# Two heads' attention products in turns behind the later one, first query blocks joined, and the final norm's row spread two weight tiles into its expert

## The chip, the cores and the metric

The kernel runs on one core of a Trainium2 chip. TensorE (PE) multiplies matrices and accumulates in PSUM banks; VectorE (DVE) and ScalarE (ACT) empty the banks and do the elementwise work; the queues of SyncE (SP), ACT and GpSimd (POOL) issue the DMA transfers. The metric is the device time of one execution in microseconds; the median over several executions counts.

## What is computed

The input is 512 tokens of 1024 numbers in fp32. Two blocks follow each other. The first has two layers, of which the first is a causal attention with a forget gate, the second a gated linear recurrence; each is normed and followed by a gated projection. The second block has three mixers side by side, a long convolution, an attention over a neighbourhood on a grid and a pooling, and after them sixteen experts that each take the 64 tokens that score highest. A last norm with the gain `final_g` ends it. Cut to what the change touches:

```python
def fox_attention(q, k, v, c):            # 16 heads of 64, 512 positions
    def block(i):                         # query block of 128
        s = einsum('bhqd,bhkd->bhqk', qb, k) * scale
        s = s + (cb[..., :, None] - c[..., None, :])
        s = where(kpos <= qpos, s, -inf)
        w = softmax(s)
        return einsum('bhqk,bhkd->bhqd', w, v)
...
def neighbourhood_attention(q, k, v, rpb): # 8 heads of 64, grid of 8 rows by 64
    s = einsum('bchd,bicjhd->bhcij', q_row, k_nb) + bias   # 8 rows by 16 columns
    p = softmax(s over the neighbourhood)
    return einsum('bhcij,bicjhd->bchd', p, v_nb)
...
y = silu(xs @ w_gate[e]) * (xs @ w_up[e]) @ w_down[e]      # 16 experts
return rms_norm_2(x, final_g)
```

## The kernel before

**Dense projections.** `group` runs a projection in pieces. Weights and inputs are split into two numbers each, and `mm3` (L326 to L330) issues three products of 128 by 512 for each pair of tiles into one of four accumulator banks `acc`. `group` has an argument `fill`: a list of steps that are called between its products, evenly spread. All attention work stands in such lists. Engines run their instructions in program order; a scheduler of the framework sets that order, by the priority that code written earlier has and by when it thinks operands and buffers are ready. `high_priority` and `issue_after` steer it.

**First attention (`fox_body`).** Heads go in pairs, head a = 0 on partitions 0 to 63 and a = 1 on 64 to 127. For each pair and each of four query blocks, `unit(b, i)` (L577) takes two score banks `sc`, issues three products for head 0, then three for head 1 (L591), adds the causal mask through one product each (L594), and then for each head: DVE adds the bias row `cb` and finds the maximum (L599), ACT takes the exponential (L600), DVE the reciprocal and the scaling (L601, L602). The bias rows come by DMA on ACT's queue at the pair's first unit, into two buffers. `turn` (L605) transposes the weights `so` into a bank `pt` (L615) and ACT copies them out (L617). `avs` (L619) multiplies with the values for both heads, four products each of 512 down to 128 columns (L624), and DVE copies the bank `oT` out. `heads` (L629) makes steps of this: step k holds unit k, `avs` of a pair whose last turn is done, and the turn of unit k - 1. Two lists of four pairs are spread over five projections (L656 to L664).

**Second attention (`second_body`, L1072).** `na(b, jp)` (L1108) does one unit from end to end, for two heads and two of four column groups: four score products in two banks (L1115), then for each head in turn the bias addition with maximum (L1126), the sign (L1128), the exponential (L1130), the reciprocal (L1131), the scaling (L1133), four transposes (L1137), ACT's copy `pt` (L1139), and four products with the values (L1143), two halves of 128 positions for each of two column groups. DVE copies the bank `oN` to `YN` (L1147). Four of the eight units fill the projection `qk1`; the other four follow after two mixers' outputs are scaled and split (`into`), so that they lie beside the products of the output projection.

**Experts (`moe_body`).** A weight tile is 2 MB. `load` (L1448 to L1467) issues the tiles on SP's queue; the first twelve go to buffers that the mixers before leave free one by one, then a ring of them is refilled as each tile is used. `up(e)` (L1577) uses eight tiles, gate (`g`) and up (`u`) in alternation (L1587); behind the last product of tile `at`, counted from 0, it hangs small work: from `at` 4 the `scatter` of the expert before (`st`, L1648, added to the tokens' rows by DVE, L1649), and in expert 14 at 5 and 6 `gains` (L1633), which spreads one half of the row final_g over 128 partitions by a product with ones (`fg`, L1637) into a bank that `scatter` also uses. `down` (L1620) has the products with the third matrix. The last expert's products of that kind are issued in quarters (L1695).

## Time and profile before

| | |
|---|---|
| median of 3 executions | 1881.55 us (1879.29 to 1884.54) |
| the profiled execution | 1878.07 us, its span 1876.3 us |
| mean granted TensorE clock | 0.996 |
| busy: PE, DVE, ACT | 1818.5 us (97%), 846.6 us (45%), 494.6 us (26%) |
| DMA traffic | 496.94 MB, mean 265 GB/s |
| chain that ended last | PE 80%, DMA 13%, DVE 5% |

The profile is of one execution. The span runs from the first to the last instruction. Busy time is the sum of an engine's instructions; the records of PE overlap each other, so that starts are the better measure of its pace. A window row gives the busy time of each engine in a stretch with the number of instructions, then the granted clock and the DMA engines' mean share; with a tile, of that tile's instructions alone. In a timeline the number behind x says how many records one row joins, and a bracket tells idle time just before and what ended it.

### The profile page before, as it was taken

The numbers are of one execution on the slowest core, as the hardware profiler recorded it, in microseconds if no ns is written. First come the engines' busy times: TensorE is split into PE (matmuls) and PEld (weight loads), VectorE is DVE, ScalarE is ACT, GpSimd is POOL, SyncE is SP. The second block draws the span as 40 slices with busy tenths as digits, with TensorE's granted clock in tenths as the row PEclk, the third lists the DMA queues.
The fourth block names the chain that finished last, engine by engine and source line by source line (L and its number), as shares of the span: only waits on it lengthen the run. The fifth ranks groups of instructions, "written<-read, shape, count | busy, mean of one in ns | idle before, by whom it ended". The sixth has DMA issues, their size and how long they took to land.

```text
span 1876.3 us, 21770 instructions
## 1 busy us (share of the span) xinstructions
PE 1818.5 (97%) x8672; PEld 1036.2 (55%) x8672; DVE 846.6 (45%) x1946; ACT 494.6 (26%) x869; POOL 23.5 (1%) x37
## 2 busy tenths in 40 slices
PE   9999999999999999999999999999999989999897
PEld 6767677888888888776743333333333332333232
DVE  6464667774735574767532213333212331133212
ACT  6454644462434454235401000000000000000002
POOL 0000000000000000000100000000000000000000
PEclk9999999999999999999999999999999999999999
DMA  5322143322221337333899999999999999999995
GB/s 167 111 79 90 57 132 132 101 96 90 65 70 57 113 97 242 102 113 104 319 413 403 422 428 428 426 428 429 427 428 426 428 428 428 428 426 428 428 419 187
DMA packets 61403, 496.94 MB, mean 265 GB/s; under 512 B 7161, under 2 KB 8313, under 8 KB 36459
## 3 DMA queue, kind: packets, MB, share of 16 engines
q1 hardware_dynamic: 51908, 470.46, 62.1%
q10 hardware_dynamic: 7592, 18.70, 3.0%
q0 software_dynamic: 1792, 6.29, 1.1%
q8 instruction: 70, 1.15, 0.2%
q14 instruction: 41, 0.34, 0.1%
HBM read 491.20 MB, written 4.23 MB: 264 GB/s over the span
## 4 chain that ended last, share of the span: by engine, by line
PE 80%; DMA 13%; DVE 5%; ACT 1%; issue 1%; SPq 0%; ACTq 0%; DVEq 0%
PE acc L328 12%; PE acc L329 11%; PE acc L330 11%; DMA w<-mu 11%; PE y L1627 10%; PE u L1587 8%; PE g L1587 7%; PE gx L1539 3%; PE st L1648 2%; DMA w<-mg 1%; PE hT L1614 1%; PE oT L624 1%; PE sc L591 1%; PE pt L615 1%; PE oT L779 1%; PE oN L1143 1%
## 5 line engine op out<-in xcount | busy, mean ns | idle before, releaser
L328 PE MATMUL acc<-xhi,whi 128*128 128x512 f32 x800 | 318.2, 401 | 0.7 <-ACT xhi L323 0.7
L1649 DVE TENSOR_TENSOR H<-H,st 128x512 f32<-128x512 f32 x120 | 78.1, 683 | 522.0 <-PE st L1648 522.0
L330 PE MATMUL acc<-xhi,wlo 128*128 128x512 f32 x800 | 313.3, 393 | 0.0
L329 PE MATMUL acc<-xlo,whi 128*128 128x512 f32 x784 | 308.2, 393 | 0.2 <-DVE xlo L324 0.2
L1587 PE MATMUL g<-w,xt 128*64 128x512 f32 x1024 | 261.7, 598 | 11.2 <-DMA w<-mg 11.1
L1587 PE MATMUL u<-w,xt 128*64 128x512 f32 x1008 | 246.9, 596 | 8.7 <-DMA w<-mu 8.3
L306 DVE TENSOR_TENSOR wlo<-wraw,whi 128x1024 fp32r<-128x1024 f32 x127 | 155.1, 1222 | 180.9 <-ACT whi L305 159.7
L1627 PE MATMUL y<-w,ZH 128*64 128x512 f32 x944 | 222.9, 594 | 0.0
L305 ACT ACTIVATE whi<-wraw 128x1024 fp32r<-128x1024 f32 x127 | 134.2, 1057 | 210.8 <-PE acc L329 141.1
L1587 PEld LDWEIGHTS g<-w,xt 128*64 128x64 f32 x1024 | 79.9, 137 | 165.6 <-issue 137.9
L328 PEld LDWEIGHTS acc<-xhi,whi 128*128 128x128 f32 x800 | 150.4, 188 | 36.1 <-issue 3.4
L330 PEld LDWEIGHTS acc<-xhi,wlo 128*128 128x128 f32 x800 | 150.6, 188 | 31.8 <-issue 1.6
L329 PEld LDWEIGHTS acc<-xlo,whi 128*128 128x128 f32 x784 | 147.5, 188 | 32.1 <-issue 3.6
L1587 PEld LDWEIGHTS u<-w,xt 128*64 128x64 f32 x1008 | 74.3, 137 | 152.2 <-issue 129.1
L1627 PEld LDWEIGHTS y<-w,ZH 128*64 128x64 f32 x944 | 69.4, 137 | 130.5 <-issue 128.7
L1604 ACT ACTIVATE gs<-g 128x512 f32<-128x512 f32 x32 | 19.1, 597 | 389.9 <-PE g L1587 361.1
L1539 PE MATMUL gx<-res,oh 128*64 128x256 f32 x512 | 62.3, 385 | 10.8 <-DVE H L1649 10.8
L1571 ACT ACTIVATE ZH<-ogT 128x512 f32<-128x512 f32 x16 | 9.6, 597 | 228.0 <-PE ogT L1569 228.0
L1648 PE MATMUL st<-ZH 64*128 64x512 f32 x240 | 67.7, 641 | 0.0
L328 PE MATMUL acc<-whi,xhi 128*128 128x512 f32 x160 | 64.5, 404 | 0.0
L330 PE MATMUL acc<-whi,xlo 128*128 128x512 f32 x160 | 62.8, 392 | 0.0
L329 PE MATMUL acc<-wlo,xhi 128*128 128x512 f32 x160 | 62.8, 392 | 0.0
(510 smaller groups left out, 1934.8 us busy)
## 6 DMA issues: line engine op xcount, KB each, us to landing
w<-mg SPq DMA_DIRECT2D x63, 2048.0 KB, 32.2
w<-mu SPq DMA_DIRECT2D x62, 2048.0 KB, 31.2
w<-md SPq DMA_DIRECT2D x59, 2048.0 KB, 35.1
wraw<-wg SPq DMA_DIRECT2D x115, 512.0 KB, 3.5
w<-md SPq DMA_DIRECT2D x16, 512.0 KB, 10.8
cb<-cd ACTq DMA_DIRECT2D x16, 256.0 KB, 3.6
wraw<-wg POOLq DMA_DIRECT2D x8, 512.0 KB, 3.8
nab<-nab ACTq DMA_DIRECT2D x12, 256.0 KB, 2.9
```

What stands on the lines that cost most here:

```text
L305: self.last = nc.scalar.activation(hi, w, AF.Copy)
L306: nc.vector.tensor_sub(lo, w, hi.bitcast(F32))
L328: mm(out, wh, xh, start=start, stop=False)
L329: mm(out, wh, xl, start=False, stop=False)
L330: mm(out, wl, xh, start=False, stop=stop)
L591: nc.tensor.matmul(ss[a][:, :n], x[sl, i * 128:n], y[sl, :n], start=y is kh and x is qh, stop=False, skip_group_check=True)
L1539: nc.tensor.matmul(Q[w][t * 64:t * 64 + 64, :256], oh[:, i, :], rv[:, i, t, w], start=i == 0, stop=i == 3, skip_group_check=True)
L1587: mm = nc.tensor.matmul(A[b][t * 64:t * 64 + 64, :], xt[:, 2 * i + k, :], w[:, c:c + 512], start=at < 2 and k == 0, stop=at > 5 and k == 1 ...
L1604: nc.scalar.activation(g, G[b], AF.Silu)
L1627: nc.tensor.matmul(Y[t * 64:t * 64 + 64, :], hT[:, i % 2 * 4 + k, i // 2, :], w[:, k, t * 512:t * 512 + 512], start=kk == 0, stop=kk == 15 ...
L1648: nc.tensor.matmul(q, OHT[e][sl, i * 128:i * 128 + 128], YY[e][sl, :], start=True, stop=True)
L1649: V.tensor_add(total[:, i, t * 512:t * 512 + 512], total[:, i, t * 512:t * 512 + 512], q)
```

## The change

A new helper `pairs` takes a list of products, issues the first, and the rest only behind it. Both attentions now list the products of two heads alternately, head 1 first; softmax and transposes go through head 0 first.

In the first attention, query blocks 0 and 1 are one unit: block 0 takes the first 128 columns of a bank, block 1 the next 256; one mask product covers both diagonal squares. A pair has three units, a list of four pairs 14 steps where it had 18, and the lists are cut anew over the projections. Softmax and transposes still go by head and block, one at a time.

In the second attention `na` is cut in three: `scores`, `turn` and `values`. Step k issues the scores of unit k, the values of unit k - 2 and the transposes of unit k - 1; the values' eight products are one list over both heads. `so` lies in the tiles `t2` (five buffers) and no longer in one of its own (two). There are ten steps; 4 and 5 now stand between the two `into` of the first half of the output projection.

`gains` is called in expert 14 behind tiles 1 and 2, and no longer behind 5 and 6.

```diff
+    def pairs(self, todo):
+
+        mm = self.nc.tensor.matmul
+        (a, k), *todo = todo
+        first = mm(*a, skip_group_check=True, **k)
+        with self.tc.issue_after(first.ins):
+            for a, k in todo:
+                mm(*a, skip_group_check=True, **k)
+
...
+        STEPS = (0, 1), (2,), (3,)
+
+        def unit(b, g):
 
             (qh, ql), (kh, kl) = QT[b], KT_[b]
-            n = 128 * (i + 1)
...
             ss = [self.sc(), self.sc()]
-            for a in range(2):
-                sl = slice(a * 64, a * 64 + 64)
-                for x, y in ((qh, kh), (qh, kl), (ql, kh)):
-                    nc.tensor.matmul(ss[a][:, :n], x[sl, i * 128:n], y[sl, :n], start=y is kh and x is qh, stop=False,
-                                     skip_group_check=True)
-            for a in range(2):
-                nc.tensor.matmul(ss[a][:, i * 128:n], self.identb, self.cmask, start=False, stop=True, skip_group_check=True)
+            at = {i: 128 * (i - STEPS[g][0]) for i in STEPS[g]}
+            todo = []
+            for x, y in ((qh, kh), (qh, kl), (ql, kh)):
+                for i in STEPS[g]:
+                    n = 128 * (i + 1)
+                    for a in (1, 0):
+                        sl = slice(a * 64, a * 64 + 64)
+                        todo.append(((ss[a][:, at[i]:at[i] + n], x[sl, i * 128:n], y[sl, :n]), dict(start=y is kh and x is qh and i == STEPS[g][0], stop=False)))
+            self.pairs(todo)
+            for a in (1, 0):
+                if g == 0:
+                    nc.tensor.matmul(ss[a].rearrange("p (j k) -> p j k", k=128)[:, 0:3:2, :], self.identb,
+                                     self.cmask[:, None, :].to_broadcast([128, 2, 128]), start=False, stop=True, skip_group_check=True)
+                else:
+                    nc.tensor.matmul(ss[a][:, g * 128 + 128:g * 128 + 256], self.identb, self.cmask, start=False, stop=True, skip_group_check=True)
             with self.tc.high_priority():
                 for a in range(2):
-                    so = fp.tile([128, 512], F32, name="so", tag="so", bufs=4)
-                    st = fp.tile([128, 4], F32, name="st", tag="st", bufs=6)
-                    nc.vector.tensor_tensor_reduce(so[:, :n], ss[a][:, :n], CB[b][a][:, :n], 1.0, 3.0e38, OP.add, OP.min, st[:, 0:1])
-                    nc.scalar.activation(so[:, :n], so[:, :n], AF.Exp, bias=st[:, 0:1], scale=-1.0, accum_out=st[:, 1:2])
-                    nc.vector.reciprocal(st[:, 2:3], st[:, 1:2])
-                    nc.vector.tensor_scalar(so[:, :n], so[:, :n], st[:, 2:3], None, op0=OP.mult)
-                    SO[b, i, a] = so
-
...
                 t = self.tp("pt")
-                for j in range(i + 1):
-                    m = i - j if a else j
-                    nc.tensor.transpose(t[:, m * 128:(m + 1) * 128], so[:, j * 128:(j + 1) * 128], self.ident)
-                p = PTS[b][:, 15 - 5 * i::6, :][:, :i + 1, :] if a else PTS[b][:, i + 1::5, :][:, :i + 1, :]
-                nc.scalar.activation(p, t[:, :128 * (i + 1)].rearrange("p (j q) -> p j q", q=128), AF.Copy)
+                for i in STEPS[g]:
+                    at = i - STEPS[g][0]
+                    for j in range(i + 1):
+                        m = at + (i - j if a else j)
+                        nc.tensor.transpose(t[:, m * 128:(m + 1) * 128], so[:, (at + j) * 128:(at + j + 1) * 128], self.ident)
+                    p = PTS[b][:, 15 - 5 * i::6, :][:, :i + 1, :] if a else PTS[b][:, i + 1::5, :][:, :i + 1, :]
+                    nc.scalar.activation(p, t[:, at * 128:(at + i + 1) * 128].rearrange("p (j q) -> p j q", q=128), AF.Copy)
 
         def avs(b):
             o = self.av("oT")
+            todo = []
             for j in range(4):
-                for a in range(2):
+                for a in (1, 0):
                     hd = 2 * b + a
-                    nc.tensor.matmul(o[a * 64:a * 64 + 64, j * 128:], v[:, j, hd * 64:hd * 64 + 64],
-                                     PTS[b][:, 15 - 5 * j:19 - 6 * j, :] if a else PTS[b][:, 6 * j + 1:5 * j + 5, :],
-                                     start=j == 0, stop=j == 3, skip_group_check=True)
+                    todo.append(((o[a * 64:a * 64 + 64, j * 128:], v[:, j, hd * 64:hd * 64 + 64],
+                                  PTS[b][:, 15 - 5 * j:19 - 6 * j, :] if a else PTS[b][:, 6 * j + 1:5 * j + 5, :]),
+                                 dict(start=j == 0, stop=j == 3)))
+            self.pairs(todo)
...
-            us = [(b, i) for b in bs for i in range(4)]
+            us = [(b, g) for b in bs for g in range(3)]
 
             def step(k):
                 if k < len(us):
                     unit(*us[k])
-                if k > 1 and us[k - 2][1] == 3:
+                if k > 1 and us[k - 2][1] == 2:
                     avs(us[k - 2][0])
...
-        self.group(X, "av0", "N", evv(0), hs[:4])
-        self.group(X, "aq1", "T", evq(1), hs[4:11])
-        self.group(X, "av1", "N", evv(1), hs[11:])
+        self.group(X, "av0", "N", evv(0), hs[:3])
+        self.group(X, "aq1", "T", evq(1), hs[3:8])
+        self.group(X, "av1", "N", evv(1), hs[8:])
         self.group(X, "ak1", "T", evk(1))
         hs = heads(4, 5, 6, 7)
-        self.group(X, "ag0", "T", evg(0), hs[:9])
-        self.group(X, "ag1", "T", evg(1), hs[9:])
+        self.group(X, "ag0", "T", evg(0), hs[:7])
+        self.group(X, "ag1", "T", evg(1), hs[7:])
...
-        def na(b, jp):
+        SO, PTS = {}, {}
+        units = [(b, jp) for b in range(4) for jp in range(2)]
+
+        def scores(b, jp):
 
             ss = [self.sc(), self.sc()]
+            todo = []
             for jj in range(2):
                 j = 2 * jp + jj
-                for a in range(2):
+                for a in (1, 0):
                     sl = slice(a * 64, a * 64 + 64)
-                    nc.tensor.matmul(ss[a][:, jj * 256:jj * 256 + 256], QT[b][sl, j, :],
-                                     KT_[b][sl, NAW[j] * 8:NAW[j] * 8 + 256],
-                                     start=True, stop=True, skip_group_check=True)
-            o = self.av("oN")
+                    todo.append(((ss[a][:, jj * 256:jj * 256 + 256], QT[b][sl, j, :], KT_[b][sl, NAW[j] * 8:NAW[j] * 8 + 256]),
+                                 dict(start=True, stop=True)))
+            self.pairs(todo)
...
-                so = tile_("so")
+                so = SO[b, jp, a] = t2("so")[:, :512].rearrange("p (a k) -> p a k", a=2)
...
+        def turn(b, jp):
+
+            for a in range(2):
+                sf = SO.pop((b, jp, a)).rearrange("p a k -> p (a k)")
                 t = self.tp("pt")
-                sf = so.rearrange("p a k -> p (a k)")
                 for i in range(4):
                     nc.tensor.transpose(t[:, i * 128:i * 128 + 128], sf[:, i * 128:i * 128 + 128], self.ident)
-                pt = tile_("pt")
+                pt = PTS[b, jp, a] = tile_("pt")
                 nc.scalar.activation(pt, t, AF.Copy)
-                hd = 2 * b + a
-                for jj in range(2):
-                    for hf in range(2):
-                        nc.tensor.matmul(o[a * 64:a * 64 + 64, jj * 128:jj * 128 + 128],
-                                         vw[:, 2 * (2 * jp + jj) + hf, hd * 64:hd * 64 + 64],
-                                         pt[:, jj * 256 + hf * 128:jj * 256 + hf * 128 + 128], start=hf == 0, stop=hf == 1,
-                                         skip_group_check=True)
+
+        def values(b, jp):
+
+            o = self.av("oN")
+            pts = [PTS.pop((b, jp, a)) for a in range(2)]
+            todo = []
+            for jj in range(2):
+                for hf in range(2):
+                    for a in (1, 0):
+                        hd = 2 * b + a
+                        todo.append(((o[a * 64:a * 64 + 64, jj * 128:jj * 128 + 128], vw[:, 2 * (2 * jp + jj) + hf, hd * 64:hd * 64 + 64],
+                                      pts[a][:, jj * 256 + hf * 128:jj * 256 + hf * 128 + 128]), dict(start=hf == 0, stop=hf == 1)))
+            self.pairs(todo)
...
+        def na(k):
+
+            if k < len(units):
+                scores(*units[k])
+            if k > 1:
+                values(*units[k - 2])
+            if 0 < k <= len(units):
+                turn(*units[k - 1])
 
...
-        def nas(*us):
-            return [lambda b=b, j=j: na(b, j) for b, j in us]
+        def nas(*ks):
+            return [lambda k=k: na(k) for k in ks]
 
         self.group(X, "hz", "T", evh)
         self.group(X, "hp", "T", evp, [lambda: zt(0), lambda: zt(1), lambda: spectrum(1)])
         self.group(X, "qk0", "T", evqk(0), [lambda: spectrum(0)])
         self.group(X, "qk1", "T", evqk(1), [lambda: inverse(0), lambda: inverse(1), lambda: normed(YP, 2, sqp, "pl")] +
-                   nas((0, 0)) + [lambda: normed(YH, 2, sqh, "hy")] + nas((0, 1), (1, 0), (1, 1)))
+                   nas(0) + [lambda: normed(YH, 2, sqh, "hy")] + nas(1, 2, 3))
         MA, MB = ((m[:, 0:4, :], m[:, 4:8, :]) for m in self.X2())
         into(MA, 0, YP, 6)
         into(MA, 2, YH, 0)
+        for f in nas(4, 5):
+            f()
         into(MB, 0, YN[:, 0:2, :], 2)
-        for f in nas((2, 0), (2, 1), (3, 0), (3, 1)):
+        for f in nas(6, 7, 8, 9):
             f()
         into(MB, 2, YN[:, 2:4, :], 4)
...
-                    if e == 14 and 4 < at < 7:
-                        gains(at - 5)
+                    if e == 14 and 0 < at < 3:
+                        gains(at - 1)
```

In these listings an instruction is a row with its line, operation, output<-input and columns; x4 stands for four in a row. In the changed kernel attention's products stand on the lines of `pairs`, L330 (the first) and L333 (the rest); `mm3` is on L337 to L339. First TensorE in the first attention, where a pair's first unit is issued; before:

```order
L591 MATMUL sc<-kh,qh 128x128
L328 MATMUL acc<-xhi,whi 128x512
L329 MATMUL acc<-xlo,whi 128x512
L330 MATMUL acc<-xhi,wlo 128x512
L591 MATMUL sc<-kl,qh 128x128
L591 MATMUL sc<-kh,ql 128x128
L591 MATMUL sc<-kh,qh 128x128
L591 MATMUL sc<-kl,qh 128x128
L591 MATMUL sc<-kh,ql 128x128
L594 LDWEIGHTS identb
L594 MATMUL sc<-cmask,identb 128x128
L594 LDWEIGHTS identb
L594 MATMUL sc<-cmask,identb 128x128
L615 MATMUL pt<-ident,so 128x128 x4
```

and with the change:

```order
L330 MATMUL sc<-kh,qh 128x128
L333 MATMUL sc<-kh,qh 128x128
L333 MATMUL sc<-kh,qh 128x256 x2
L333 MATMUL sc<-kl,qh 128x128 x2
L333 MATMUL sc<-kl,qh 128x256 x2
L333 MATMUL sc<-kh,ql 128x128 x2
L333 MATMUL sc<-kh,ql 128x256 x2
L609 LDWEIGHTS identb
L609 MATMUL sc<-cmask,identb 128x2x128
L609 LDWEIGHTS identb
L609 MATMUL sc<-cmask,identb 128x2x128
L637 MATMUL pt<-ident,so 128x128 x4
```

The unit of block 0 stood with its first product apart from its other five. Now twelve products of both blocks and heads stand together, the masks are two rows of two squares, and nothing lies between.

TensorE in the second attention, where the fill of `qk1` has begun to use values; before:

```order
L328 MATMUL acc<-xhi,whi 128x512
L1143 MATMUL oN<-pt,vw 64x128 x4
L1137 MATMUL pt<-ident,so 128x128 x4
L329 MATMUL acc<-xlo,whi 128x512
L330 MATMUL acc<-xhi,wlo 128x512
L1115 MATMUL sc<-k,q 128x256
L1143 MATMUL oN<-pt,vw 64x128 x4
L380 MATMUL nrm<-ones,sqhy 128x1 x4
L1115 MATMUL sc<-k,q 128x256
L328 MATMUL acc<-xhi,whi 128x512
L1115 MATMUL sc<-k,q 128x256 x2
L329 MATMUL acc<-xlo,whi 128x512
```

and with the change:

```order
L339 MATMUL acc<-xhi,wlo 128x512
L330 MATMUL sc<-k,q 128x256
L1168 MATMUL pt<-ident,t_6553 128x128 x4
L333 MATMUL sc<-k,q 128x256 x2
L330 MATMUL oN<-pt,vw 64x128
L333 MATMUL oN<-pt,vw 64x128 x7
L1168 MATMUL pt<-ident,t_6610 128x128 x4
L333 MATMUL sc<-k,q 128x256
L337 MATMUL acc<-xhi,whi 128x512
L338 MATMUL acc<-xlo,whi 128x512
```

Each head's four products with the values were a piece of their own, and a unit's scores stood in three places. Now the values of two heads are one piece of eight, behind their first; this unit's scores are still in three pieces.

TensorE in expert 14, at the products `fg` that spread final_g; before:

```order
L1587 MATMUL u_10929<-w_10913,xt 64x512 x2
L1587 MATMUL u_10930<-w_10913,xt 64x512 x2
L1648 MATMUL st<-ZH 128x512 x2
L1637 MATMUL fg<-w_10690,ones 128x512
L1587 MATMUL g_10927<-w_10915,xt 64x512 x2
L1587 MATMUL g_10928<-w_10915,xt 64x512 x2
L1587 MATMUL g_10927<-w_10915,xt 64x512 x2
L1587 MATMUL g_10928<-w_10915,xt 64x512 x2
L1648 MATMUL st<-ZH 128x512 x2
L1637 MATMUL fg<-w_10690,ones 128x512
L1587 MATMUL u_10929<-w_10917,xt 64x512 x2
```

and with the change:

```order
L1635 MATMUL u_10866<-w_10841,xt 64x512 x2
L1635 MATMUL u_10865<-w_10841,xt 64x512 x2
L1635 MATMUL u_10866<-w_10841,xt 64x512 x2
L1685 MATMUL fg<-w_10626,ones 128x512
L1635 MATMUL g_10863<-w_10843,xt 64x512 x2
L1635 MATMUL g_10864<-w_10843,xt 64x512 x2
L1635 MATMUL g_10863<-w_10843,xt 64x512 x2
L1635 MATMUL g_10864<-w_10843,xt 64x512 x2
L1685 MATMUL fg<-w_10626,ones 128x512
```

Each `fg` stood behind a pair of `st`, the scatter's products. Now it stands between the weight products of tiles 1 and 2, 2 and 3, with no scatter near.

## Rows read from the trace of the kernel before

**Rows 1.** The page's part 2, tenths of 40 slices of 46.9 us; DMA is the engines' busy share.

```profile
PE   9999999999999999999999999999999989999897
DMA  5322143322221337333899999999999999999995
```

**Rows 2.** Timeline of SP's queue: start us, us, engine line op out<-in.

```profile
949.51 0.33 SPq L1467 DMA_DIRECT2D w<-md  x1
```

**Rows 3.** Timeline of PE in expert 14: start us, us, engine, line; [idle before <-releaser].

```profile
1755.20 3.65 PE L1587 MATMUL g<-w,xt 128*64 128x512 f32 x16 [1.24 <-DMA w<-mg]
...
1766.56 1.27 PE L1637 MATMUL fg<-w,ones 1*128 1x512 f32 x2 [1.43 <-DVE H L1649]
...
1767.76 5.16 PE L1587 MATMUL g<-w,xt 128*64 128x512 f32 x16
...
1774.75 1.12 PE L1637 MATMUL fg<-w,ones 1*128 1x512 f32 x2 [0.78 <-DVE H L1649]
...
1775.80 1.51 PE L1587 MATMUL u<-w,xt 128*64 128x512 f32 x6
```

**Rows 4.** Timeline of PE, a run of 48 projection products.

```profile
903.65 0.39 PE L328 MATMUL acc<-xlo,whi 128*128 128x512 f32 x1
...
914.56 0.39 PE L328 MATMUL acc<-mn,whi 128*128 128x512 f32 x1
```

**Rows 5.** Windows, tile acc: stretch, us, PE, PEld, DVE, ACT busy (x), PEclk, DMA share, GB/s.

```profile
60.00:260.00 200.00, 142.10 (x544) 97.34 (x543) 8.12 (x12) 5.43 (x8) 1.00 0.25 80
```

**Rows 6.** Timeline of PE, one pair of heads in the first attention.

```profile
92.65 2.37 PE L624 MATMUL oT<-PT,v 128*64 128x512 f32 x16
...
97.95 0.39 PE L330 MATMUL acc<-xhi,wlo 128*128 128x512 f32 x1
...
115.46 0.40 PE L330 MATMUL acc<-xhi,wlo 128*128 128x512 f32 x1
```

**Rows 7.** Timeline of PE, score units of the first attention.

```profile
77.48 0.51 PE L591 MATMUL sc<-kh,qh 64*128 64x512 f32 x2
...
78.39 0.28 PE L594 MATMUL sc<-cmask,identb 128*128 128x128 bf16 x2
...
86.89 0.32 PE L591 MATMUL sc<-kh,qh 64*128 64x128 f32 x1
```

**Rows 8.** Timeline of DVE, first attention.

```profile
242.92 0.29 DVE L599 CUSTOM_DVE_ANT_0 so<-sc,cb 128x128 f32<-128x128 f32 x1 [2.90 <-DMA cb<-cd]
```

**Rows 9.** Windows of 820 to 898 us: all (PE, PEld, DVE, ACT, POOL), then tile acc.

```profile
820.00:898.00 78.00, 77.63 (x411) 54.87 (x410) 49.69 (x166) 43.74 (x103) 2.66 (x5) 1.00 0.41 141
820.00:898.00 78.00, 41.01 (x143) 24.35 (x142) 6.38 (x8) 0.00 (x0) 1.00 0.41 141
```

**Rows 10.** Timeline of PE, second attention.

```profile
820.96 1.13 PE L1115 MATMUL sc<-k,q 64*128 64x256 f32 x8
...
822.02 0.50 PE L328 MATMUL acc<-xhi,whi 128*128 128x512 f32 x1
...
829.83 1.09 PE L1143 MATMUL oN<-pt,vw 128*64 128x128 f32 x8
...
830.85 0.66 PE L1137 MATMUL pt<-ident,so 128*128 128x128 f32 x4
...
831.89 0.70 PE L1115 MATMUL sc<-k,q 64*128 64x256 f32 x2
...
832.52 1.09 PE L1143 MATMUL oN<-pt,vw 128*64 128x128 f32 x8
...
844.45 1.13 PE L1115 MATMUL sc<-k,q 64*128 64x256 f32 x4
```

**Rows 11.** Windows, all engines, around the products of final_g.

```profile
1764.00:1772.00 8.00, 6.57 (x22) 1.99 (x22) 4.04 (x17) 0.60 (x1) 0.00 (x0) 0.79 1.01 430
```

**Rows 12.** Windows, all engines, the end of the weight stream.

```profile
1844.00:1848.00 4.00, 4.00 (x22) 1.36 (x20) 0.00 (x0) 0.00 (x0) 0.00 (x0) 1.00 0.59 218
```

**Rows 13.** Timeline of PE, the last products on weights.

```profile
1854.77 5.37 PE L1695 MATMUL y<-w,ZH 128*64 128x512 f32 x24
```

More of the change, by code (lines that the diff above doesn't have):

```diff
@@ L575, in fox_body @@
         PTS, CB, SO = {}, {}, {}
-        def unit(b, i):
+        STEPS = (0, 1), (2,), (3,)
+        def unit(b, g):
             (qh, ql), (kh, kl) = QT[b], KT_[b]
-            n = 128 * (i + 1)
-            if i == 0:
+            if g == 0:
                 CB[b] = []
@@ L602, in unit @@
-                    nc.vector.tensor_scalar(so[:, :n], so[:, :n], st[:, 2:3], None, op0=OP.mult)
-                    SO[b, i, a] = so
-        def turn(b, i):
-            if i == 0:
+                    so = SO[b, g, a] = fp.tile([128, 512], F32, name="so", tag="so", bufs=4)
+                    for i in STEPS[g]:
+                        n = 128 * (i + 1)
+                        sl = slice(at[i], at[i] + n)
+                        st = fp.tile([128, 4], F32, name="st", tag="st", bufs=6)
+                        nc.vector.tensor_tensor_reduce(so[:, sl], ss[a][:, sl], CB[b][a][:, :n], 1.0, 3.0e38, OP.add, OP.min, st[:, 0:1])
+                        nc.scalar.activation(so[:, sl], so[:, sl], AF.Exp, bias=st[:, 0:1], scale=-1.0, accum_out=st[:, 1:2])
+                        nc.vector.reciprocal(st[:, 2:3], st[:, 1:2])
+                        nc.vector.tensor_scalar(so[:, sl], so[:, sl], st[:, 2:3], None, op0=OP.mult)
@@ L609, in turn @@
+        def turn(b, g):
+            if g == 0:
                 PTS[b] = fp.tile([128, 20, 128], F32, name="PT", bufs=1)
             for a in range(2):
-                so = SO.pop((b, i, a))
+                so = SO.pop((b, g, a))
                 t = self.tp("pt")
-                for j in range(i + 1):
-                    m = i - j if a else j
-                    nc.tensor.transpose(t[:, m * 128:(m + 1) * 128], so[:, j * 128:(j + 1) * 128], self.ident)
-                p = PTS[b][:, 15 - 5 * i::6, :][:, :i + 1, :] if a else PTS[b][:, i + 1::5, :][:, :i + 1, :]
@@ L617, in turn @@
-                nc.scalar.activation(p, t[:, :128 * (i + 1)].rearrange("p (j q) -> p j q", q=128), AF.Copy)
+                for i in STEPS[g]:
+                    at = i - STEPS[g][0]
[4 more added lines that the diff above has]
+                    nc.scalar.activation(p, t[:, at * 128:(at + i + 1) * 128].rearrange("p (j q) -> p j q", q=128), AF.Copy)
@@ L1084, in t2 @@
         def t2(name="t2"):
-            return sp.tile([128, 544], F32, name=name, tag="t2", bufs=5)
+            return tile_("t2")
         def evqk(g):
```

3 lines of the change are left out of this document (2 added, 1 removed).

## The prediction

> **What bounds the kernel now.** I read the page's forty slices first, then stretches of the timeline on TensorE and on SP's queue, then sums over windows. The slices [rows 1] show two regimes. Up to about 910 us TensorE is busy without a gap and the DMA engines are mostly a tenth to a half full. From there to about 1844 us the DMA engines are full, because sixteen experts bring their weights. The second regime starts where the first one lets it: the first expert's loads go into buffers that the mixers free one after another, and the ring's refill is issued at 949.51 [rows 2], just after TensorE's first gate products. So TensorE time saved before about 910 us moves the whole weight stream and the end with it, one for one. Behind the last wait for weights, at 1755.20 [rows 3], TensorE alone leads to the end. In the stretches that the change touches, then, TensorE's time is the currency. One projection product costs (914.56 - 903.65) / 48 = 0.2273 us [rows 4]; what a stretch holds beyond its projection products is attention.
>
> **The change part by part.**
>
> *First attention.* The stretch from 60 to 260 us holds eight pairs of heads and 544 projection products [rows 5], 544 x 0.2273 = 123.7 us, so attention costs at most 200 - 123.7 = 76.3 us. One whole pair with 39 projection products around it runs from 97.95 to 115.46 [rows 6]: 17.51 - 39 x 0.2273 = 8.65 us, and 8 x 8.65 = 69.2. The other 7.1 us go into pieces broken up by the order and into short waits. Two parts of the edit act here.
> Turns: the two heads' products are queued 0, 0, 0, 1, 1, 1 and yet each stands in the timeline as a record of two that run at once, all six and a transition in 78.39 - 77.48 = 0.91 us [rows 7]. Taking turns has nothing to win in a whole unit. [...]
> Joint units: blocks 0 and 1 become one unit, so a pair has three score pieces and three pieces of transposes where it had four of each. What one entry into such a piece costs no row shows by itself; the nearest is the shortest product, alone at 86.89, 0.32 us long for 128 columns [rows 7], which stream in a quarter of rows 4's 0.2273, 0.06 us. Between 0 and 0.32 per pair and kind I take 0.35 for both kinds together, 8 x 0.35 = 2.8 us. The causal mask's columns stay as many. Of the 7.1 us in broken pieces and waits, the new order breaks three score units of 24 where the old one broke five of 32, and fewer of the transposes and values; I count 3.2 of the 7.1 as gone. Together **6 us**. Bounds: 2 us if the joints alone count, at less than I took; 9 us if nearly all the 7.1 go too.
> DVE, ACT and the bias rows' loads keep their counts per head and lie beside TensorE, which has no gap there. If that cover went, a late bias row would cost what DVE waits for one today, 2.90 us [rows 8].
>
> *Second attention.* From 820 to 898 us there are 143 projection products [rows 9], 32.5 us of 78, so this attention with its neighbours costs about 45 us. Values: today each head's four products are a piece by themselves, 830.85 - 829.83 = 1.02 us [rows 10], sixteen of them, 16.3 us. The first attention's values, where both heads alternate, took 2.37 us for 2 x 1280 columns [rows 6], 0.95 us for the 2 x 512 here. Eight pieces at 1.0 us are 8.2, so 8.1 us go. Scores: a unit left whole takes 822.02 - 820.96 = 1.06 us, a piece of two products of one head shows the same 1.13 us record at 844.45, a lone product takes 832.52 - 831.89 = 0.63 [rows 10]. The old order has nine pieces of two to four products and nine lone ones: 9 x 1.06 + 9 x 0.63 = 15.2 us. The new one has five whole units, three pieces of two products, now of different heads, which I put at a lone product's time, and six lone ones: 5 x 1.06 + 9 x 0.63 = 11.0, so 4.2 go (3 if the pairs cost 1.06). Scores and values together have eleven pieces fewer, and each entry saved at some 0.14 us (by the same estimate as above) is another 1.5. TensorE's part is 8.1 + 4.2 + 1.5 = 13.8 us.
> What lies beside it may not fit. DVE is busy for 49.69 of these 78 us [rows 9]. Of its 155 instructions in the stretch, 144 still stand between the first bias addition and the last in the new order, 46 us in proportion. TensorE has 73 projection products there (16.6 us) and some 21 us of attention, 38 in all. So DVE ends later than TensorE in part of the stretch, and TensorE then waits at a score bank or an unfinished transpose. I give back 3 of the 13.8 us: **11 us**. Bounds: 4, if DVE's 46 and a chain behind it set the pace all the way, and 16, if nothing is given back and the projections fill better.
> The Trainium skill ("TensorEngine Tiling (Array Packing)", Performance Considerations, PSUM Bottleneck) warns that packing speeds TensorE and not the emptying of PSUM. DVE's 49.69 in rows 9 agrees that it can bite here; by the rule alone the gain would be near that lower bound, and the sum 1866 or 1867 us.
>
> *Last norm's row.* The two products that spread final_g stand in the next to last expert's sixth and seventh weight tiles, behind the scatter. There TensorE waits 1.43 and 0.78 us for a bank that DVE empties, the products take 1767.76 - 1766.56 = 1.20 and 1775.80 - 1774.75 = 1.05, and the gate products between them take 5.16 instead of 3.65 us [rows 3]: the granted clock is 0.79 there [rows 11], in mean between its levels 1.2 and 2.4 GHz, after the engine had stood 1.43 us. Sum: 1.43 + 0.78 + 1.20 + 1.05 + 1.51 = 6.0 us. Behind the second and third tile, where the change puts them, TensorE is waiting for weights (1.24 us at 1755.20), no scatter stands ahead, and 1.05 to 1.2 us each fit into such a wait. They cost nothing if the wait is there. The last pieces of weights land near 1846 to 1848 us (the DMA share falls to 0.59 there [rows 12]) and the last products that need them start at 1854.77 [rows 13], so about 6 us of slack lie between. Gain **5 us** (3 if the last expert's first tiles come too late, 6 in full).
>
> *Everything else* (tiles from one pool instead of another, values held one step longer) costs no instruction. Ring refills and loads are issued behind the same TensorE instructions as before, so they come earlier by what TensorE gains.
>
> **Sum.** 6 + 11 + 5 = 22 us. The profiled execution took 1878.07 us, which gives 1856.1; it lies 3.5 us under the median 1881.55 of the runs, so the forecast for the median is 1881.55 - 22 = **1859.5 us**. About 0.3%, 5.6 us, is what a measurement of this kernel can tell from no change.
>
> **Rivals.**
> - *DVE becomes the bound of the second attention* (chance 0.17). For: 49.69 of 78 us busy, and a chain addition, maximum, exponential, reciprocal, scaling behind every unit. Against: scores are now queued two units ahead of their values. The attention then gives 0 to 4, I take 2: 6 + 2 + 5 = 13, 1868.5 us.
> - *Order counts in the first attention too* (0.07). If products of two heads ran at once only where they stand next to each other, the old score units would take five turns (of six products one pair overlaps) and the new ones three. Two turns of 1280 columns, at 0.2273 us per 512, are 1.14 us per pair, 9.1 in all: 1850.4 us. [...] Against: rows 7.
> - *The last expert's transfers absorb the norm row's move* (0.08). The stream ends when it ends; if TensorE gets there early it waits for the last tiles: 1859.5 + 5 = 1864.5 us. Against: rows 12 and 13.
> - *The queue stands behind the first product* (0.05), slower. Whatever product needs the later bank goes first and everything else stands behind it on TensorE, projections too: 24 units in the first attention, 8 in the second. If eight first units each wait 2.90 us for the bias row's addition [rows 8] and the eight of the second 1.06 us (a unit's own length) for DVE, that is 23.2 + 8.5 = 31.7 us: 1891 us. It decides from 22 / 32 = 0.7 us per unit, and is slower beyond no change from 0.86. Against: nothing idles on TensorE before 910 us today.
> - *The change does not do what it says* (0.03): values of two heads in turns don't run at once in pieces as short as these, stay at 1.02 us per head, and 8.1 us fail to come: 1867.6 us. Against: the first attention's 2.37 us [rows 6].
>
> **How the numbers follow.** The forecast has 0.60, with a range of its own of 1854 to 1866 from the bounds above. The range takes in DVE's rival on the one side and the strict order's on the other: 1849 to 1873 us, which leaves out the slower case, half of the strict order's, the tail of DVE's and the ends of the forecast's own, 2 in 10 at most. Faster by over 0.3% (under 1875.9) 0.90: all cases but the queue's and the tail of DVE's; within 0.3% 0.06, from that tail and short waits of the queue; slower 0.04, from long ones.
>
> **What would show it.** In the profile after: the eight value pieces of the second attention at about 1.0 us each for both heads; its stretch from the first score to the last value shorter by 11 us; idle of TensorE there put down to DVE, up to 4 us, and more if DVE's rival holds; score records of the first attention still near 0.9 us for the last block, hence nothing from turns; the ring's refill issued at about 949.5 - 17 = 932.5 us; no wait for DVE ahead of the final_g products, the gate products there at 3.65 us; the end 22 us earlier. It is wrong if TensorE idles on the score banks in the first attention, if the DMA engines have gaps between 900 and 1840 us, or if the stretch from that refill to the end is longer.

## The result and the profile after

The changed kernel takes **1861.43 us** (median of 4 executions, 1860.91 to 1862.17) where the kernel before took 1882.18 beside it (median of 4): ratio 0.9891, 95% interval 0.9874 to 0.9908, 20.7 us less. The forecast was 1859.5 us. Its profiled execution took 1860.99 us, 17.1 less than the profiled one of before, which lies 4.1 us under its median. One execution of the changed kernel in the last run below took 6395.35 us and stands in no median here.

The two regimes are the same, part 2 of the page after, against [rows 1]:

```profile
PE   9999999999999999999999999999999989999997
DMA  4322233222121226335799999999999999999996
```

To see where the time went I counted TensorE's 3072 projection products from 0 through each trace and took the start of four of them, the last wait of an expert's product for its weights, and the first product `base<-ZH` of the end. Between them lie the stretches. "Changed, again" is a second trace of the changed kernel, from the last run below.

| stretch of TensorE, us | before | changed | changed, again |
|---|---|---|---|
| products 200 to 750, first attention | 261.25 - 59.50 = 201.75 | 258.99 - 61.13 = 197.86 | 197.97 |
| products 750 to 2800, no change there | 547.24 | 548.36 | 551.27 |
| products 2800 to 2990, second attention | 906.85 - 808.49 = 98.36 | 893.90 - 807.35 = 86.55 | 86.57 |
| product 3071 to the last wait for weights | 828.71 | 830.43 | 829.54 |
| from there to the end's first `base` | 105.64 | 99.71 | 99.70 |

So 3.9 us came from the first attention, 11.8 from the second and 5.9 from expert 14; the weight stream lost 1.7, the stretch without a change 1.1, and the time before product 200 another 1.6 (a fall of the clock, in the last section). Together that is, but for rounding, the 17.1 us between the two profiled executions. Add up each record's time until the next record starts, by the kind of product, and the attentions open up:

| us (pieces) | before | changed |
|---|---|---|
| first attention: scores and masks | 28.64 (38) | 26.69 (30) |
| first attention: values | 20.70 (10) | 18.59 (9) |
| second attention: scores | 15.14 (18) | 12.39 (14) |
| second attention: values | 16.29 (16) | 8.58 (9) |

The changed kernel's 26.69 us hold 0.92 in which TensorE stands. Its waits from 60 to 262 us, first before, then changed; the view of waits gives the total, the number of waits and the longest:

```profile
PE pt L615 <- ACT PT L617: 0.5, 1, 0.5
PE pt L615 <- DVE so L602: 0.2, 1, 0.2
```

```profile
PE pt L637 <- DVE so L623: 0.9, 1, 0.9
PE pt L637 <- ACT PT L639: 0.8, 1, 0.8
PE pt L637 <- DVE st L622: 0.3, 1, 0.3
```

The transposes of the first attention wait 2.0 us in all where they waited 0.7.

The second attention's values, timeline of TensorE in the changed kernel, against the one-head pieces of [rows 10]:

```profile
831.08 1.13 PE L333 MATMUL sc<-k,q 64*128 64x256 f32 x4
832.14 0.50 PE L337 MATMUL acc<-xhi,whi 128*128 128x512 f32 x1
...
836.08 0.70 PE L333 MATMUL sc<-k,q 64*128 64x256 f32 x4
836.84 0.32 PE L330 MATMUL oN<-pt,vw 128*64 128x128 f32 x1
836.84 0.32 PE L333 MATMUL oN<-pt,vw 128*64 128x128 f32 x1
837.00 0.27 PE L330 MATMUL oN<-pt,vw 128*64 128x128 f32 x1
837.00 0.93 PE L333 MATMUL oN<-pt,vw 128*64 128x128 f32 x13
837.86 0.66 PE L1168 MATMUL pt<-ident,t 128*128 128x128 f32 x4
```

The first product (L330) and the first of the rest (L333) start together: two heads run at once. Eight products take 837.86 - 836.84 = 1.02 us, as four of one head did. (An fp32 product has two records.) The scores' pieces of two products show both prices: 836.84 - 836.08 = 0.76 us where they are of different heads and 832.14 - 831.08 = 1.06 where they run one after the other.

What TensorE waits for from 810 to 900 us in the changed kernel:

```profile
PE acc L338 <- DVE xhi L324: 0.5, 1, 0.5
PE sc L330 <- DVE k L1121: 0.2, 1, 0.2
```

Nothing there is a wait for a softmax. In expert 14 the products of final_g stand where weights are awaited, against [rows 3]:

```profile
1732.85 1.12 PE L1685 MATMUL fg<-w,ones 1*128 1x512 f32 x2
1734.17 3.65 PE L1635 MATMUL g<-w,xt 128*64 128x512 f32 x16 [0.20 <-DMA w<-mg]
...
1737.75 1.12 PE L1685 MATMUL fg<-w,ones 1*128 1x512 f32 x2
1739.06 3.65 PE L1635 MATMUL u<-w,xt 128*64 128x512 f32 x16 [0.18 <-DMA w<-mu]
...
1743.95 3.65 PE L1635 MATMUL g<-w,xt 128*64 128x512 f32 x16 [1.24 <-DMA w<-mg]
```

Behind each of them 0.2 us of the wait are left of the 1.24 that the next tile shows. They cost nothing.

The loss in the weight stream stands at the ring's refill, on SP's queue against [rows 2], with the window of 4 us at it, first before, then changed:

```profile
936.54 0.33 SPq L1515 DMA_DIRECT2D w<-md  x1
```

```profile
948.00:952.00 4.00, 4.00 (x22) 1.40 (x20) 0.00 (x0) 0.00 (x0) 0.00 (x0) 1.00 0.81 283
```

```profile
936.00:940.00 4.00, 4.00 (x22) 1.35 (x20) 0.00 (x0) 0.00 (x0) 0.00 (x0) 1.00 0.65 193
```

The refill comes 13.0 us earlier, and the DMA engines are less full around it, 0.65 against 0.81 of 4 us: the transfers issued from the mixers' side seem to be through before TensorE's first gate products give tiles back. It is so in every trace: in the first 4 us behind product 3071 the share is 0.62 to 0.68 in the eleven with the new second attention and 0.81 to 0.87 in the three with the old one.

### The profile page after: what moved, and what is told of

It reads as the page before. It is cut to its first block, busy times and chain, and to the rows that moved or that the text cites. A ratio compares the mean times of both kernels' runs of the same rounds, so it can differ in the third digit from the quotient of the medians.

```text
span 1859.2 us, 21731 instructions
## 1 busy us (share of the span) xinstructions
PE 1801.0 (97%) x8656; PEld 1024.2 (55%) x8656; DVE 842.6 (45%) x1946; ACT 494.4 (27%) x869; POOL 23.6 (1%) x37
## 4 chain that ended last, share of the span: by engine, by line
PE 76%; DMA 17%; DVE 5%; ACT 1%; issue 1%; SPq 0%; ACTq 0%; DVEq 0%
DMA w<-mu 15%; PE acc L337 11%; PE acc L338 11%; PE y L1675 11%; PE acc L339 11%; PE u L1635 8%; PE g L1635 6%; PE gx L1587 3%; PE st L1696 2%; DMA wraw<-wg 1%; PE hT L1662 1%; PE pt L637 1%; DVE wlo L306 1%; PE sc L333 1%; PE oT L803 1%
## 5 line engine op out<-in xcount | busy, mean ns | idle before, releaser
L337 PE MATMUL acc<-xhi,whi 128*128 128x512 f32 x800 | 318.1, 400 | 1.9 <-ACT xhi L323 1.8
L339 PE MATMUL acc<-xhi,wlo 128*128 128x512 f32 x800 | 314.2, 394 | 0.0
L337 PEld LDWEIGHTS acc<-xhi,whi 128*128 128x128 f32 x800 | 150.8, 189 | 38.5 <-issue 3.6
L339 PEld LDWEIGHTS acc<-xhi,wlo 128*128 128x128 f32 x800 | 150.6, 188 | 31.1 <-issue 0.7
L337 PE MATMUL acc<-whi,xhi 128*128 128x512 f32 x160 | 64.3, 403 | 0.0
L339 PE MATMUL acc<-whi,xlo 128*128 128x512 f32 x160 | 62.9, 393 | 0.0
```

What stands on the lines that cost most here:

```text
L337: mm(out, wh, xh, start=start, stop=False)
L339: mm(out, wl, xh, start=False, stop=stop)
```

## The experiments

**The parts by themselves.** Three kernels are before with one part of the change each; the fourth is the changed kernel with the last part undone. The first attention alone:

```diff
+        STEPS = (0, 1), (2,), (3,)
...
+            self.pairs(todo)
```

> Before with the first attention's part alone (joint units, turns, new steps). Theory: the parts add up, and the traces of before and after show 3.9 us less between the start of the first and the end of the last unit of that attention (63 to 260 us), of which about 1 us is lost again up to 760 us: 3 to 4 us faster than before. By the forecast's own term it would be 6 us. Rival, strict program order: 10 us or more.

Measured 1875.71 us against 1881.57 (ratio 0.9970, 0.9957 to 0.9982), 5.9 us. In its trace the first attention's stretch is 198.09 us, as in the changed kernel, the second's 98.38, as before. The stretch gives 3.7 us, within the theory's 3 to 4; the median gives more.

The second attention alone:

```diff
-        def na(b, jp):
+        def scores(b, jp):
...
+        def values(b, jp):
```

> Before with the second attention's part alone (scores, transposes and values in steps, values of both heads in turns). Theory: 11.8 us less on TensorE there, as between the traces of before and after, less 1 to 2 us that the weight stream loses where the ring is refilled: 10 to 12 us faster than before. Rival, DVE sets the pace when the first attention is not changed too: 0 to 4 us.

Measured 1867.96 us (0.9929, 0.9903 to 0.9956), 13.6 us, more than the theory's 10 to 12; its stretch is 86.61, 11.8 us less. DVE does not set the pace.

The row of final_g alone:

```diff
-                    if e == 14 and 4 < at < 7:
-                        gains(at - 5)
+                    if e == 14 and 0 < at < 3:
+                        gains(at - 1)
```

> Before with the two products of final_g alone moved to tiles 1 and 2 of expert 14. Theory: 5.9 us faster, the two waits (1.43, 0.78), the two products (2.25) and the slow gate products (1.51) gone. Rival, the last weights absorb it: 0 to 2 us. If the slow clock at these products was chance and not of the wait, 4.4 us.

Measured 1874.03 us (0.9961, 0.9949 to 0.9974), 7.5 us, more than the theory's 5.9; in its trace the end's stretch is 101.24 us, 4.4 less. The changed kernel with this edit undone:

> The changed kernel with the products of final_g back at tiles 5 and 6. Theory, parts independent: 4.4 to 6 us slower than the changed kernel, that is about 14 to 16 us faster than before; the sum of the two runs of the attentions' parts alone. Rival, the parts overlap: clearly less or more than that sum.

Measured 1865.41 us (0.9912, 0.9886 to 0.9937), 16.2 us under before and 4.0 over the changed kernel. Its timeline in expert 14:

```profile
1744.76 3.65 PE L1635 MATMUL g<-w,xt 128*64 128x512 f32 x16 [1.24 <-DMA w<-mg]
...
1756.12 1.12 PE L1685 MATMUL fg<-w,ones 1*128 1x512 f32 x2 [1.42 <-DVE H L1697]
1757.17 3.65 PE L1635 MATMUL g<-w,xt 128*64 128x512 f32 x16
...
1762.66 1.12 PE L1685 MATMUL fg<-w,ones 1*128 1x512 f32 x2 [0.77 <-DVE H L1697]
1763.71 3.65 PE L1635 MATMUL u<-w,xt 128*64 128x512 f32 x16
```

The same two waits, 1.42 and 0.77 us, and yet the gate products between them take 3.65 us, not the 5.16 of [rows 3]. In the kernel with the second attention alone they are slow again:

```profile
1755.82 1.12 PE L1670 MATMUL fg<-w,ones 1*128 1x512 f32 x2 [1.33 <-DVE H L1682]
1756.87 5.35 PE L1620 MATMUL g<-w,xt 128*64 128x512 f32 x16
```

The kernel with the row's move alone had no wait at these products, and slow gate products two tiles later, behind a wait for weights:

```profile
1747.84 1.12 PE L1637 MATMUL fg<-w,ones 1*128 1x512 f32 x2
...
1752.47 1.12 PE L1637 MATMUL fg<-w,ones 1*128 1x512 f32 x2
...
1759.17 5.35 PE L1587 MATMUL g<-w,xt 128*64 128x512 f32 x16 [1.99 <-DMA w<-mg]
```

So the slow clock follows these waits in two of the four traces with the products at their old place, before and the second attention alone (end's stretch 105.64 and 105.68 us), and not in the other two, this kernel and the first attention alone (103.99 each). At the new place the stretch is 99.71: 4.3 us without the slow clock, which is 1.42 + 0.77 + 1.05 + 1.05, and 5.9 with it. What decides whether it comes, no run shows.

The medians of the three parts add up to 27.0 us, the change brought 20.7, while the stretches in the traces add up part by part. What the medians hold besides is below, under the hardware.

**Values by head.** The second attention's values in one piece, but head 1's four and then head 0's four:

```diff
-            for jj in range(2):
-                for hf in range(2):
-                    for a in (1, 0):
+            for a in (1, 0):
+                for jj in range(2):
+                    for hf in range(2):
```

> The changed kernel with the second attention's values one head after the other (head 1's four products, then head 0's, still in one piece). The stretch from the first to the last projection product around that attention (between products 2800 and 2990) took 98.4 us before and 86.6 with the change. Theory, the turns bring the values' 8 us: a piece takes 2.04 us and not 1.02, the stretch 94 to 95. Rival, standing together is enough, as the first attention's scores ran at once though queued head by head: the stretch stays at 86.6 and only the new steps count.

Measured 1864.53 us, the stretch 89.85, between the two: both theories were wrong in part. Timeline of TensorE:

```profile
839.06 0.43 PE L330 MATMUL oN<-pt,vw 128*64 128x128 f32 x2
839.33 1.31 PE L333 MATMUL oN<-pt,vw 128*64 128x128 f32 x14
840.58 0.66 PE L1168 MATMUL pt<-ident,t 128*128 128x128 f32 x4
```

A piece takes 1.52 us. All values take 12.42 us, against 16.29 before and 8.58 in turns: about half of the gain is from standing together, half from turns.

**The division left out.** Without the 32 scalings on DVE the second attention's weights stay undivided:

```diff
-                nc.vector.reciprocal(st[:, 2:4], st[:, 2:4])
-                for jj in range(2):
-                    nc.vector.tensor_scalar(so[:, jj, :], so[:, jj, :], st[:, 2 + jj:3 + jj], None, op0=OP.mult)
```

> The changed kernel without the division of the second attention's softmax (its 32 scalings on DVE left out, 9.9 us of DVE; the weights stay undivided). Theory, DVE costs TensorE nothing but broken score units: the new order has ten score pieces and not fourteen, worth 1 to 1.5 us, so the stretch goes from 86.6 to about 85.3. Rival, DVE sets the pace as the forecast's 3 us given back say: 83.6 or less.

Measured 1858.83 us, the stretch 84.48, 2.1 us less. The scores alone went from 12.39 us in 14 pieces to 10.27 in 10, which is all of it, and TensorE's waits did not get fewer (1.4 us from 810 to 900, with the division 0.7). DVE's work costs TensorE no idle time in this attention; it costs through the order that the scheduler writes for it. The price is somewhat above my 1.5, the mechanism the theory's.

**One step for a unit.** Scores, transposes and values called in one go again, values still in turns:

```diff
             if k < len(units):
                 scores(*units[k])
-            if k > 1:
-                values(*units[k - 2])
-            if 0 < k <= len(units):
-                turn(*units[k - 1])
+                turn(*units[k])
+                values(*units[k])
```

> The changed kernel with scores, transposes and values of a unit in one step again, the values of both heads still in turns. Theory, turns carry the gain and the steps little: the stretch stays within 1 us of 86.6, since the scheduler finds other products to put between. Rival, the steps keep TensorE from waiting: values wait for ACT's copy, and the stretch goes half the way back, to 90 or more, with idle time put down to ACT or DVE.

Measured 1859.22 us (0.9903, 0.9874 to 0.9932), the stretch 84.36: 2.2 us better than with steps, which neither theory had. Waits from 810 to 900 us, the only one:

```profile
PE acc L338 <- DVE xhi L324: 0.2, 1, 0.2
```

The scores take 11.21 us in 12 pieces and the values 8.21, all eight whole. That is 1.5 of the 2.2 us; the rest is in the products around. The scheduler already puts other products between the parts of a unit, and the steps broke more pieces. Timed again with the changed kernel on the same chip:

> The kernel of the run with one step for a unit of the second attention, timed against before and, in the same call, beside the changed kernel. Theory, its stretch is 2.2 us shorter and the weight stream gives back half: 1 to 2.2 us faster than the changed kernel, in the median. Rival, the weight stream takes all of it: the same.

> The changed kernel itself once more, beside the kernel with one step. Theory: 1861 us, 20 us under before, and a second trace with the stages of the first (197.9 and 86.6 us). Where the slow clock falls is open: if it falls at 28 us again, it belongs to this kernel; if not, it is chance.

1858.55 us (0.9874, 0.9853 to 0.9894) against 1859.69 (median of three; 0.9876, 0.9851 to 0.9902), before 1881.60. The traces repeat the stretches: 84.37 and 86.57. The version with one step is the better one by its trace, by 2.2 us; the medians point the same way, by 1.1 us, within their intervals. The clock did not fall at 28 us again in the changed kernel.

**Head 0 first.** All lists of products begin with head 0, in four places and at the mask; one of them:

```diff
...
-                    for a in (1, 0):
+                    for a in (0, 1):
...
```

> The changed kernel with head 0 first in all lists of products. In the order seven of eight value pieces of the second attention then stand as 1 + 7 products, with other work between, and little else moves. Theory, that head 1 comes first is what keeps the pieces whole: each break costs 0.3 to 0.5 us, the stretch goes from 86.6 to 89 or 90. Rival, a lone product costs next to nothing: 86.6.

Measured 1861.14 us, the stretch 87.80, 1.25 us more, where the theory had 2.4 to 3.4. Timeline of TensorE:

```profile
835.43 0.43 PE L330 MATMUL oN<-pt,vw 128*64 128x128 f32 x2
...
837.28 1.09 PE L333 MATMUL oN<-pt,vw 128*64 128x128 f32 x14
838.30 0.66 PE L1168 MATMUL pt<-ident,t 128*128 128x128 f32 x4
```

The seven products left take 1.02 us, as eight would, and the lone one comes on top. Values cost 10.67 us, 2.1 more; the scores, whole more often, give 0.5 back, and the rest is in the products around. The rule that the rest is issued behind the first changes nothing: without it the order of the whole program is the same, instruction for instruction. What keeps the second attention's pieces whole is that the list begins with the head whose operands come last. In the first attention it counts less: the values take 19.22 us there, 0.6 more than with head 1 first.

**First attention by head.**

```diff
-            for x, y in ((qh, kh), (qh, kl), (ql, kh)):
-                for i in STEPS[g]:
...
-                    for a in (1, 0):
+            for a in (1, 0):
+                for x, y in ((qh, kh), (qh, kl), (ql, kh)):
+                    for i in STEPS[g]:
...
-            for j in range(4):
-                for a in (1, 0):
+            for a in (1, 0):
+                for j in range(4):
```

> The changed kernel with the first attention's lists by head: all of head 1's score products of a unit, then head 0's, and the values likewise. The stretch between projection products 200 and 750 took 201.7 us before and 197.9 with the change. Theory, from the run of the second attention's values by head (a piece 1.52 us, between 1.02 in turns and 2.04 apart): the overlap of two heads reaches over a few products only; the values' pieces go from 2.3 to about 3.4 us, 8 or 9 us in all, and the scores of three products a head stay as they were. The stretch would be 206 or 207. Rival, only standing together counts here: 197.9.

Measured 1875.59 us (0.9963, 0.9952 to 0.9974), the stretch 213.36: 15.5 us more. Values went from 18.59 to 31.00 us, scores from 26.69 to 30.07. Timeline of TensorE:

```profile
95.08 1.07 PE L330 MATMUL oT<-PT,v 128*64 128x512 f32 x2
95.99 3.02 PE L333 MATMUL oT<-PT,v 128*64 128x384 f32 x14
98.94 0.33 PE L637 MATMUL pt<-ident,so 128*128 128x128 f32 x1
```

These eight take 98.94 - 95.08 = 3.86 us by head. In turns, in the changed kernel:

```profile
96.24 0.64 PE L330 MATMUL oT<-PT,v 128*64 128x512 f32 x1
96.25 0.64 PE L333 MATMUL oT<-PT,v 128*64 128x512 f32 x1
96.72 0.59 PE L330 MATMUL oT<-PT,v 128*64 128x512 f32 x1
96.73 1.89 PE L333 MATMUL oT<-PT,v 128*64 128x512 f32 x13
98.55 0.33 PE L637 MATMUL pt<-ident,so 128*128 128x128 f32 x1
```

98.55 - 96.24 = 2.31 us. The theory's direction holds and its size was too small. It also had the scores staying as they were: those of three products a head do (1.03 us by head, 1.02 in turns, a last block's unit with its masks), but the joined unit has six a head and goes from 1.12 to 1.45.

**Four units a pair.**

```diff
-        STEPS = (0, 1), (2,), (3,)
+        STEPS = (0,), (1,), (2,), (3,)
...
```

> The changed kernel with four units for a pair of heads in the first attention again, turns and head 1 first kept. Between before and the changed kernel the scores there took 1.8 us less and the values 2.1 us less. Theory, the joints bring the scores' part alone: the stretch goes from 197.9 to 199.7 or 200. Rival, the joints bring all of it (fewer steps, so that the values stay whole): 201.7.

Measured 1861.28 us, the stretch 199.60. The joints bring 1.7 us by the traces, which the medians don't show, nearly all in the scores (28.17 against 26.69 us). Without the 0.92 us in which TensorE stands the scores gain 2.4; its waits in the stretch are 1.0 us here and 2.0 with the joints. The values, 18.43 us in eight whole pieces, kept their gain without the joints. Which part of the edit their gain is from stays open: in the run with head 0 first, which has the joints, they still kept 1.5 of the 2.1 us.

## Why the prediction was right, step by step

The sign, the largest part and the path, TensorE's time before the weights, were right; the sum of 22 us stands against 20.7. That the time came within 1.9 us of the forecast is in part luck: between the profiled executions the gain is 17.1, and the rest is the distance of each from its median, 4.1 us before and 0.4 after. The two smaller parts came in the other order. The terms:

- **First attention, 6 us: 3.8 measured.** The joints were put at 2.8 and bring 1.7: 2.4 in the scores, less 1.0 of new waits, and the rest around. The prediction had DVE and ACT lie beside a TensorE without a gap; that cover failed here, if only by 1.3 us. The 3.2 counted back from broken pieces are 2.1 in the values, 1.8 of it from two of eight pieces that stood broken before, one of which still does. The sentence that turns have nothing to win held for the old units of three products a head, [rows 7], but not beyond: by head, the joint units and the values of the changed kernel cost 15.5 us. The prediction had it as a rival that order counts; it saw no time for it in this change only because the values went in turns already.
- **Second attention, 11 us: 11.8.** Values were put at 8.1 and gave 7.7 (one piece stayed broken); scores at 4.2 with a lower bound of 3 and gave 2.75. That pieces of two products would be of different heads held for one of three; the other two are of one head and take 1.06 us, and one whole unit, queued head by head, takes 1.53. Fewer pieces, 1.5, are 1.3, which is what is left over and was not measured by itself. The 3 us given back to DVE were not taken: TensorE waits 0.7 us there in all. The step that failed is the one from DVE's 46 us to a wait of TensorE. (The share of 155 instructions behind the 46 does not fit [rows 9], which count 166; by these it is 43.) DVE's work of one unit lies beside the products of others, and its price showed in the order alone. So 11 came near 11.8 by luck: the 3 us not taken stand against 2.0 that the other terms fell short.
- **Row of final_g, 5 us: 4.3, or 5.9 with the slow clock.** The waits and products are as put. The 1.51 us of slow clock in the sum come in some executions and not in others.
- **Weights follow TensorE one for one:** nearly. From product 3071 to the last wait for weights it takes 828.0 to 828.9 us, 828.5 in the mean, in the three traces with the old second attention and 828.7 to 830.4, 829.3 in the mean, in the eleven with the new one: about 0.8 us stays behind, as much as the DMA share that is lower by 0.2 in the 4 us behind product 3071 leaves undone. No run tested this by itself. The refill came at 936.54 us and not at 932.5: the first attention gave 2.1 us less than put and the second 0.8 more, and 2.7 were lost before product 200 and in the stretch without a change.
- **The rivals.** DVE as the bound fell with the second attention alone. The last weights absorbing the row's move fell with the end's stretch, 4.3 us shorter. The queue behind the first product: the changed kernel shows no wait of that kind above 0.2 us (with four units a pair there is one of 0.5), and the rule that it hung on changes no order.

The Trainium skill ("TensorE: Matmul & The Clock Gate", Part 3, The mechanism) says that matmuls start and end strictly in program order. The traces bear that out in part: queued by head, three products a head run at once as in turns, four short ones partly (1.52 us between 1.02 and 2.04), four long ones hardly (3.86 against 2.31). The Trainium skill ("TensorEngine Tiling (Array Packing)", Performance Considerations, PSUM Bottleneck) also warns that packing speeds TensorE and not the emptying of PSUM, which may then become the bottleneck. That did not come true in the second attention, with DVE busy 49.69 of 78 us before: TensorE waits 0.7 us there.

## What to carry to other kernels

Where two products use different halves of the array, queue them in turns and put them into one piece, and begin the list with the one whose operands come last; in the second attention a first product otherwise went ahead alone and cost 0.36 us each time. Before splitting a chain into steps by hand, look whether the engine waits at all: here the scheduler had filled the gaps, and the steps cut pieces. A median against a kernel whose clock falls at scattered places can hold more than the edit; compare stretches between the same instructions in two traces.

## What the runs showed of the hardware

TensorE's clock falls to half, its level of 1.2 GHz, at different places in executions of one kernel. The changed kernel's first trace has such a fall at 28 us, its second none there but one at 287. Seven of the eleven traces with the new first attention fall at 28 us, none of the three with the old one; whether that is more than chance, no run shows. Windows of the first trace, then of the second (granted clock third from the end):

```profile
28.00:31.00 3.00, 3.00 (x11) 2.31 (x10) 0.16 (x1) 0.00 (x0) 0.00 (x0) 0.51 0.51 175
285.00:289.00 4.00, 4.00 (x16) 2.40 (x15) 4.00 (x7) 2.34 (x4) 0.00 (x0) 1.00 0.45 135
```

```profile
28.00:31.00 3.00, 3.00 (x17) 2.48 (x16) 0.27 (x1) 0.60 (x1) 0.00 (x0) 1.00 0.50 175
285.00:289.00 4.00, 3.57 (x8) 1.97 (x9) 2.59 (x4) 2.48 (x4) 0.00 (x0) 0.72 0.41 123
```

One fall costs 1.5 to 1.8 us where TensorE is the bound (5.16 against 3.65 in expert 14; 61.13 against 59.38 at product 200). The 39 executions of before that have a clock on record reach from 1876.61 to 1886.54 us at mean granted clocks of 0.998 to 0.992, 0.9952 in the mean; the seven of the changed kernel have 0.996 to 0.997. A difference of 0.0012 of 1880 us is 2.3 us. With it the stretches, 3.8 + 11.8 + 4.3 - 1 = 18.9, come to 21.2, about the 20.7 of the medians, and it fits that each part alone gained more in its median than in its stretch. It also fits that beside four executions of before at 0.9968, with a median of 1877.90 us, the kernel with head 0 first gained 16.8 us. That the change makes falls rarer is argued from these means; what sets off a fall was not tried.
